# The first stage of a retention and pooling layer: its low-half subtractions on VectorE, GpSimd at rest, context conditioning later

## The chip, the cores and the metric

The kernel runs on one core of a Trainium2 chip. The metric is the device time of one execution in microseconds (us), and a version of the kernel stands for the median of its runs. One execution was also recorded by the hardware profiler. Its engines are named as the profile names them: PE is the matrix engine (PEld its weight loads), DVE is VectorE, ACT is ScalarE, POOL is GpSimd, and SP is the engine that issues the DMAs.

## The reference, cut to what matters

One layer of a diffusion backbone over 512 latent tokens of width 1024, with a context of 256 tokens. The conditioning vectors `c` and `c_ctx` give a shift and a scale for each channel. The normalised tokens and the normalised context are shifted and scaled by them, and multiplied with the input projection:

```python
mod = jax.nn.silu(c) @ w_ada + b_ada
mod_c = jax.nn.silu(c_ctx) @ w_ada + b_ada
...
uc = _modulate(ctx, sh1c, sc1c)
kvc = uc @ w_in[:, :KV_COLS]
s_f, s_b = _context_states(kc, vc, lg)
u = _modulate(x, sh1, sc1)
mix = _token_mixer(u @ w_in, s_f, s_b, lg, pool_w, pool_scale, w_branch_ret, w_branch_pool, w_out)
x = _post_norm(DEEPNORM_ALPHA * x + g1 * mix, ln1_g, ln1_b)
u2 = _modulate(x, sh2, sc2)
x = _post_norm(DEEPNORM_ALPHA * x + g2 * _conv_ffn(...), ln2_g, ln2_b)
```

Of `mod` the first layer norm needs 16 tiles of 128 channels (8 shifts, 8 scales), and the rest of the layer the other 32. Of `mod_c` 16 are needed, from the same 16 tiles of `w_ada`.

## The kernel before

Every product is done with three matmuls. Each operand is held as a high half (the value rounded to the type that TensorE takes, written by ScalarE) and a low half (the value minus its high half, a subtraction on VectorE or GpSimd): high by high, high by low, low by high. All subtractions go through the helper `sub` at line 84. `split` makes both halves of a weight tile: `act.copy` at line 89, then `sub` on the engine that the caller names.

The first stage (lines 257 to 373) has eight steps, one for each block of 128 input channels (kt). A step does the 24 matmuls of line 339 that multiply that block with eight feature tiles: four of q and four of the swish gate. All eight PSUM banks (`g0`) are held until the last step. Before a step, `first_prep` makes its operands for it:

- the weights `w_first[kt]`, loaded into one of three `raw` buffers, are split into `hi` and `lo` (two buffers each);
- `first_mod` computes one shift and one scale tile of `mod`. Each is a `matvec` on VectorE (line 203: a tile of `w_ada`, 128x1024, times silu(c), summed along the row) and a small `finish_mod` (line 206);
- `modulate` (lines 215 to 221) makes the token operand: ScalarE writes the high half `uh` (line 215) and the same in full precision (line 218), and `sub` writes the low half `ul`.

The operands for step kt+1 are made ahead of the matmuls of step kt in the program. In the steps kt=4 to 7, `ctx_mod(0)` to `ctx_mod(3)` follow: each does two such sums (line 226) and two small additions for the context. In this stage all five engines keep the order of the program (`ORDS`).

Then come the steps of `run_steps`: four gate features `g_step` (called g4 to g7 here), the pooling step p0, four steps of k (k0 to k3), p1, four steps of the first half of v, p2, four of the second half, p3, and then the gates and the branches. `run_steps` calls `prep(i + 1)` ahead of the body of step i, so the weights' subtraction for the next step stands before what step i does after its matmuls. From g4 to p0, `ORD0` holds TensorE, SP and VectorE to the order of the program, while ScalarE and GpSimd follow an order chosen by the scheduler when the kernel is built. From k0 on (`ORD1`) only SP keeps the program's order.

The steps g4 to g7 also do, after their matmuls, the last four `ctx_mod`, the swish of the features (`put_g`, lines 378 to 381), the layer norm of the context (bn_stats at line 130, line 417), its transposition (line 137) and `ctx_modulate`, which needs all of them. The steps of k and v need its result. Each of these steps also loads three more tiles of `w_ada` into the `raw` buffers (`ada_tiles`) and multiplies them on VectorE (line 203 again). Their loads share the three `raw` buffers with the weights of the steps.

A pooling step copies its features, and GpSimd adds them up by doubling windows (line 459), multiplies (line 462) and subtracts. Three steps later `middle` makes the halves of the result.

Of the kernel before, what the change touches and what calls it, by code (L numbers as in the profile page):

```python
# [14 lines left out]
P = 128  # L15
# [31 lines left out]
def layer_kernel(ctx: ExitStack, tc: tile.TileContext, a: dict):  # L47
# [38 lines left out]
    def split(raw, shape, eng):  # L86
        hi = sb.tile(list(shape), F32R, tag="hi", bufs=2, name=nm("hi"))
        lo = sb.tile(list(shape), F32R, tag="lo", bufs=2, name=nm("lo"))
        act.copy(hi, raw)  # L89
        sub(eng, lo, raw, hi.bitcast(F32))  # L90
        return hi, lo
# [122 lines left out]
    def modulate(m, sh, sc, src, hi, lo, eng, also=act):  # L214
        act.activation(hi, src, AF.Identity, bias=m[:, sh:sh + 1], scale=m[:, sc:sc + 1])
        u = t2(src.shape)
        if also is act:
            act.activation(u, src, AF.Identity, bias=m[:, sh:sh + 1], scale=m[:, sc:sc + 1])
        else:
            dve.tensor_scalar(u, src, m[:, sc:sc + 1], m[:, sh:sh + 1], ALU.mult, ALU.add)  # L220
        sub(eng, lo, u, hi.bitcast(F32))
# [20 lines left out]
    def first_load(kt):  # L242
        for j in (kt, 8 + kt):
            load(ada_slot(j), a["wada"][j])
        return load(raw4((P, NF0)), a["w_first"][kt])

    def first_mod(kt):
        for j in (kt, 8 + kt):
            matvec(j, ada_slot(j), junk)
            finish_mod(mod, j, j >= 8)  # L250

    def first_prep(kt, raw):
        w = split(raw, (P, NF0), pool)
        first_mod(kt)
        modulate(mod, kt, 8 + kt, xnT[:, kt, :], uh[:, kt, :], ul[:, kt, :], pool)
        return w

    raw0 = first_load(0)
    keep("gap1", [P, 48])
# [82 lines left out]
    for kt in range(NKT):  # L342
        wh, wl = ready
        if kt == 0:
            g0 = [bank() for _ in range(4)]
            g0_mm(kt, range(0, 4), range(2))
            held += [x_trans(2, 1), x_trans(3, 1)]
            g0_mm(kt, range(0, 4), range(2, 3))
            for h in held:
                act.copy(*h)  # L350
            g0 += [bank() for _ in range(N_G0)]
            ready = split(first_load(1), (P, NF0), pool)
            first_mod(1)
            modulate(mod, 1, 9, xnT[:, 1, :], uh[:, 1, :], ul[:, 1, :], pool)
        elif kt + 1 < NKT:
            ready = first_prep(kt + 1, first_load(kt + 1))
        if kt:
            g0_mm(kt, range(0, 4))
        g0_mm(kt, range(4, 4 + N_G0))
        if kt == 1:  # L360
            silu_cc = load(row(), a["c_ctx"].broadcast_to([P, D]))
        elif kt == 2:
            for hf in range(2):
                cs = slice(hf * SEQ, (hf + 1) * SEQ)
                t = t2()
                act.activation(t, silu_cc[:, cs], AF.Sigmoid)
                dve.tensor_tensor(silu_cc[:, cs], silu_cc[:, cs], t, ALU.mult)
        if kt >= 6:
            load(ctx_raw[:, kt - 6, :], a["ctx"][(kt - 6) * P:(kt - 5) * P, :])
        if kt >= 4:  # L370
            ctx_mod(kt - 4)
    ordered(*ORD0)

    qk = slot(0, [P, 2, 4, SEQ])
# [23 lines left out]
    def ctx_trans():  # L398
        for tb in range(2):
            transpose_tb(put_ctxT, ctx_raw[:, tb, :], tb)  # L400

    def ctx_modulate():
        for kt in range(NKT):
            modulate(modc, kt, 8 + kt, ctx_nT[:, kt, :], uch[:, kt, :], ucl[:, kt, :], pool,
                     act if kt % 2 else dve)

    def g_step(h):
        def post(ps):
            if h == N_G0:
                for f in range(4):  # L410
                    act.activation(qT[:, f, :], g0[f], AF.Copy, scale=DK ** -0.5)
                for f in range(2):
                    put_g(f, g0[4 + f])
                ctx_stats = [ln_stats(ctx_raw[:, tb, :]) for tb in range(2)]
                ctx_mod(h)
                for tb, (mu, rs) in enumerate(ctx_stats):
                    dve.tensor_scalar(ctx_raw[:, tb, :], ctx_raw[:, tb, :], mu, rs, ALU.subtract, ALU.mult)
            elif h == N_G0 + 1:
                for f in range(2, N_G0):
                    put_g(f, g0[4 + f])  # L420
                ctx_mod(h)
            elif h == N_G0 + 2:
                ctx_trans()
                ctx_mod(h)
            else:
                ctx_mod(h)
                ctx_modulate()
            put_g(h, ps)

        feature_step(a["w_g"][h - N_G0], NKT, uh, ul, post, pool)  # L430

    rest = list(range(16, 48))

# [10 lines left out]

    def p_step(gi):
        def post(ps):
            invc = load(t2(), a["invc"][gi:gi + 1, :].broadcast_to([P, SEQ]))
            pad = t2((P, PADW))
            pool.memset(pad[:, 0:PADL], 0.0)
            pool.memset(pad[:, PADL + SEQ:PADW], 0.0)  # L450
            act.copy(pad[:, PADL:PADL + SEQ], ps)
            sums = [t2((P, PADW)) for _ in range(2)]
            at, lo, hi, w = pad, 0, PADW, 1
            while w < WINDOWS[gi]:
                nxt = sums[0]
                sums.reverse()
                dl, dr = (1, 0) if w == 1 else (w // 2, w // 2)
                lo, hi = lo + dl, hi - dr
                pool.tensor_tensor(nxt[:, lo:hi], at[:, lo - dl:hi - dl], at[:, lo + dr:hi + dr], ALU.add)
                at, w = nxt, 2 * w  # L460
            d = sums[0][:, 0:SEQ]
            pool.tensor_tensor(d, at[:, PADL:PADL + SEQ], invc, ALU.mult)
            sub(pool, d, d, pad[:, PADL:PADL + SEQ])
            defer(3, middle, d)

        def middle(d):
            dh, dl = t2(dt=F32R), t2(dt=F32R)
            act.copy(dh, d)
            sub(dve, dl, d, dh.bitcast(F32))
            wr = load(small([P, P]), a["pool_w"][gi])  # L470
            pw = t2((P, 2, P), F32R)
            act.copy(pw[:, 0, :], wr)
            sub(dve, pw[:, 1, :], wr, pw[:, 0, :].bitcast(F32))
            defer(1, back, dh, dl, pw)

        def back(dh, dl, pw):
            ps = bank()
            mm3(ps, pw[:, 0, :], pw[:, 1, :], dh, dl, True, True)
            o = t2()
            act.activation(o, ps, AF.Copy, scale=pscale[:, gi:gi + 1])  # L480
            act.copy(poolT[:, 0, gi, :], o)
            sub(dve, poolT[:, 1, gi, :], o, poolT[:, 0, gi, :].bitcast(F32))

        feature_step(a["w_p"][gi], NKT, uh, ul, post, dve)
# [280 lines left out]
    for h in range(N_G0, H):  # L765
        g_step(h)
    p_step(0)
    steps_k = len(steps)
    kv_steps(a["w_k"], True, k_post)
    p_step(1)  # L770
    kv_steps(a["w_v"][0], False, v_post(0))
    p_step(2)
    kv_steps(a["w_v"][1], False, v_post(1))
# [431 lines left out]
```

## Time and profile before

| | us |
|---|---|
| median of three runs | 873.96 |
| the three runs | 1165.45, 870.28, 873.96 |
| the profiled execution | 874.79 |
| its span, from its first instruction to its last | 873.0 |
| busy in the span: PE, DVE, ACT, POOL | 821.6, 624.4, 366.2, 444.2 |

The profiled execution's own time is 1.8 us longer than its span. The granted TensorE clock was 0.981 of full speed over the span. A row of the time line gives start, duration, engine, line, operation, destination and sources, how many instructions were merged, and in square brackets how long the engine had been idle before it and what ended that.

### The profile page before, as it was taken

How to read it: one execution, taken by the hardware profiler on the slowest of the kernel's cores; microseconds unless marked ns; L12 is line 12 of the kernel's file. 1: busy time of each engine (PE TensorE's matmuls, PEld its weight loads, DVE VectorE, ACT ScalarE, POOL GpSimd, SP SyncE). 2: the span in 40 equal slices, each digit the busy share in tenths (PEclk: the TensorE clock that was granted, in tenths of full speed). 3: DMA queues.
4: the chain of work that ended last, by engine and by line, in shares of the span. 5: the costliest groups of instructions: out<-in, count | busy, mean ns of one | idle time of the engine just before them, and what ended most of it. 6: DMA issues, size and time to landing. Idle time of an engine off the chain costs nothing.

```text
span 873.0 us, 10556 instructions
## 1 busy us (share of the span) xinstructions
PE 821.6 (94%) x3865; PEld 678.5 (78%) x3865; DVE 624.4 (72%) x959; ACT 366.2 (42%) x575; POOL 444.2 (51%) x304
## 2 busy tenths in 40 slices
PE   6889989999999999998998899999999998799993
PEld 4667878778888888887787898888888776688883
DVE  7899996676267773346757769999999999612138
ACT  4434544121444343233335476666655565223200
POOL 4877411121543230113456878899888886212245
PEclk9999999999999999999999999999999999999997
DMA  9932466767221104344503312222222252224202
GB/s 352 345 105 94 127 207 218 236 226 216 72 73 49 50 1 145 100 154 163 196 1 121 121 50 84 86 96 99 96 97 95 75 169 83 87 97 144 73 1 96
DMA packets 33780, 106.94 MB, mean 122 GB/s; under 512 B 4528, under 2 KB 5312, under 8 KB 33728
## 3 DMA queue, kind: packets, MB, share of 16 engines
q1 hardware_dynamic: 33728, 106.27, 35.6%
q8 instruction: 30, 0.49, 0.2%
q14 instruction: 22, 0.18, 0.1%
HBM read 104.14 MB, written 2.11 MB: 122 GB/s over the span
## 4 chain that ended last, share of the span: by engine, by line
PE 40%; DVE 39%; POOL 8%; DMA 6%; issue 5%; ACT 2%; SPq 0%; DVEq 0%; POOLq 0%; ACTq 0%
DVE t L938 19%; PE ps L96 11%; PE ps L95 11%; PE ps L94 11%; DVE S L84 4%; DMA raw<-in_wada 4%; DVE t L987 3%; POOL lo L84 3%; DVE raw L203 2%; DVE lo L84 2%; PE ps L339 1%; POOL S L84 1%; POOL sm L123 1%; PE ps L608 1%; DVE sm L130 1%
## 5 line engine op out<-in xcount | busy, mean ns | idle before, releaser
L96 PE MATMUL ps<-S,lo 128*128 128x512 f32 (+1 forms) x544 | 212.2, 392 | 5.1 <-DVE lo L84 4.7
L94 PE MATMUL ps<-S,hi 128*128 128x512 f32 (+1 forms) x544 | 213.6, 393 | 2.7 <-ACT hi L89 2.7
L95 PE MATMUL ps<-S,hi 128*128 128x512 f32 (+1 forms) x544 | 212.5, 391 | 0.2 <-POOL S L84 0.2
L84 POOL TENSOR_TENSOR lo<-raw,hi 128x1024 fp32r<-128x1024 f32 (+1 forms) x53 | 134.0, 2530 | 107.2 <-ACT hi L89 105.3
L938 DVE SCALAR_TENSOR_TENSOR t<-ps,convw,t 128x441 f32<-128x441 f32 (+1 forms) x252 | 167.6, 693 | 15.8 <-POOL t L936 11.5
L89 ACT CAST hi<-raw 128x1024 fp32r<-128x1024 f32 (+1 forms) x98 | 98.9, 1009 | 168.2 <-PE ps L95 61.7
L96 PEld LDWEIGHTS ps<-S,lo 128*128 128x128 f32 x544 | 102.8, 189 | 29.8 <-DVE lo L84 6.8
L94 PEld LDWEIGHTS ps<-S,hi 128*128 128x128 f32 x544 | 103.6, 190 | 23.7 <-ACT hi L89 3.1
L936 POOL TENSOR_TENSOR t<-t,t 128x448 f32<-128x448 f32 x88 | 116.7, 1329 | 10.0 <-ACT t L1013 6.2
L95 PEld LDWEIGHTS ps<-S,hi 128*128 128x128 f32 x544 | 103.7, 191 | 21.3 <-POOL S L84 0.6
L95 PE MATMUL ps<-S,S 128*128 128x512 f32 (+1 forms) x308 | 113.8, 370 | 5.4 <-DVE S L84 5.0
L94 PE MATMUL ps<-S,S 128*128 128x512 f32 (+1 forms) x308 | 113.1, 369 | 3.6 <-DVE t L938 3.6
L96 PE MATMUL ps<-S,S 128*128 128x512 f32 (+1 forms) x308 | 113.8, 370 | 0.2 <-POOL S L84 0.2
L84 DVE TENSOR_TENSOR lo<-raw,hi 128x1024 fp32r<-128x1024 f32 (+1 forms) x47 | 61.4, 1307 | 53.0 <-ACT hi L89 53.0
L84 POOL TENSOR_TENSOR S<-raw,S 128x1024 fp32r<-128x1024 f32 x21 | 50.8, 2423 | 68.7 <-ACT S L735 44.5
L95 PE MATMUL ps<-lo,S 128*128 128x512 f32 x208 | 81.6, 392 | 0.7 <-DVE lo L84 0.6
L96 PE MATMUL ps<-hi,S 128*128 128x512 f32 x208 | 81.3, 391 | 0.0
L94 PE MATMUL ps<-hi,S 128*128 128x512 f32 x208 | 79.2, 392 | 0.0
L95 PEld LDWEIGHTS ps<-S,S 128*128 128x128 f32 x308 | 58.9, 191 | 15.6 <-DVE S L84 5.5
L94 PEld LDWEIGHTS ps<-S,S 128*128 128x128 f32 x308 | 58.6, 191 | 13.6 <-DVE t L938 4.0
L96 PEld LDWEIGHTS ps<-S,S 128*128 128x128 f32 x308 | 58.9, 191 | 10.4 <-POOL S L84 1.1
L84 POOL TENSOR_TENSOR S<-t,S 128x512 fp32r<-128x512 f32 (+1 forms) x29 | 44.8, 1557 | 31.2 <-DVE t L220 11.1
(205 smaller groups left out, 1187.3 us busy)
## 6 DMA issues: line engine op xcount, KB each, us to landing
raw<-in_w_up SPq DMA_DIRECT2D x44, 512.0 KB, 3.3
raw<-in_wada SPq DMA_DIRECT2D x32, 512.0 KB, 4.2
raw<-in_w_down SPq DMA_DIRECT2D x22, 512.0 KB, 3.3
S<-in_wada SPq DMA_DIRECT2D x16, 512.0 KB, 6.8
raw<-in_w_first SPq DMA_DIRECT2D x8, 512.0 KB, 7.4
raw<-in_w_v SPq DMA_DIRECT2D x16, 256.0 KB, 3.3
raw<-in_w_ga SPq DMA_DIRECT2D x8, 512.0 KB, 3.4
raw<-in_w_gb SPq DMA_DIRECT2D x8, 512.0 KB, 3.3
```

The lines of the kernel that those rows point to most:

```text
L84: eng.tensor_tensor(out, x, y, ALU.subtract)
L89: act.copy(hi, raw)
L94: pe.matmul(out, lhsT=sh, rhs=mh, start=first, stop=False)
L95: pe.matmul(out, lhsT=sh, rhs=ml, start=False, stop=False)
L96: pe.matmul(out, lhsT=sl, rhs=mh, start=False, stop=last)
L123: pool.tensor_scalar(rs, mv[:, 1:2], EPS, None, ALU.add)
L130: dve.bn_stats(st[:, hf, :], src[:, hf * SEQ:(hf + 1) * SEQ])
L203: dve.scalar_tensor_tensor(out_junk, raw, 1.0, silu_c, ALU.mult, ALU.mult, accum_out=mod[:, j:j + 1])
L339: pe.matmul(g0[f], lhsT=w[:, f * P:(f + 1) * P], rhs=m[:, kt, :], start=kt == 0 and i == 0, stop=kt == NKT - 1 and i == 2)
L936: pool.tensor_tensor(o, o, i, ALU.add)
L938: dve.scalar_tensor_tensor(o, i, w, o, ALU.mult, ALU.add)
L987: dve.tensor_tensor(accs[2 * f], accs[2 * f], accs[2 * f + 1], ALU.mult)
```

## The change

In the first stage the low half of the weights and the low half of the tokens are both subtracted on VectorE, and the weights' subtraction stands behind `first_mod`. The step kt=0 keeps its own code, with its two half subtractions on GpSimd. The context conditioning `ctx_mod` leaves the first stage and the two gate steps in which it stood alone: two calls each now stand in g4, g6 and g7, and one each in p0 and p1. The context's layer norm moves from g4 to g5, its transposition from g6 to g7. `ctx_modulate` is done in three parts, in g7, p0 and p1. The weights of the gate steps are subtracted on VectorE in place of GpSimd. The pooling step p1 moves ahead of the steps of k, and so into the part where VectorE keeps the order of the program.

```diff
     def first_prep(kt, raw):
-        w = split(raw, (P, NF0), pool)
+        hi = sb.tile([P, NF0], F32R, tag="hi", bufs=2, name=nm("hi"))
+        lo = sb.tile([P, NF0], F32R, tag="lo", bufs=2, name=nm("lo"))
+        act.copy(hi, raw)
         first_mod(kt)
-        modulate(mod, kt, 8 + kt, xnT[:, kt, :], uh[:, kt, :], ul[:, kt, :], pool)
-        return w
+        sub(dve, lo, raw, hi.bitcast(F32))
+        modulate(mod, kt, 8 + kt, xnT[:, kt, :], uh[:, kt, :], ul[:, kt, :], dve)
+        return hi, lo
...
-            ready = split(first_load(1), (P, NF0), pool)
-            first_mod(1)
-            modulate(mod, 1, 9, xnT[:, 1, :], uh[:, 1, :], ul[:, 1, :], pool)
+            ready = first_prep(1, first_load(1))
...
-        if kt >= 4:
-            ctx_mod(kt - 4)
...
-    def ctx_modulate():
-        for kt in range(NKT):
+    def ctx_modulate(kts):
+        for kt in kts:
             modulate(modc, kt, 8 + kt, ctx_nT[:, kt, :], uch[:, kt, :], ucl[:, kt, :], pool,
                      act if kt % 2 else dve)
+
+    def ctx_norm():
+        ctx_stats = [ln_stats(ctx_raw[:, tb, :]) for tb in range(2)]
+        for tb, (mu, rs) in enumerate(ctx_stats):
+            dve.tensor_scalar(ctx_raw[:, tb, :], ctx_raw[:, tb, :], mu, rs, ALU.subtract, ALU.mult)
 
     def g_step(h):
         def post(ps):
             if h == N_G0:
                 for f in range(4):
                     act.activation(qT[:, f, :], g0[f], AF.Copy, scale=DK ** -0.5)
+                ctx_mod(0)
+                ctx_mod(1)
                 for f in range(2):
                     put_g(f, g0[4 + f])
-                ctx_stats = [ln_stats(ctx_raw[:, tb, :]) for tb in range(2)]
-                ctx_mod(h)
-                for tb, (mu, rs) in enumerate(ctx_stats):
-                    dve.tensor_scalar(ctx_raw[:, tb, :], ctx_raw[:, tb, :], mu, rs, ALU.subtract, ALU.mult)
             elif h == N_G0 + 1:
                 for f in range(2, N_G0):
                     put_g(f, g0[4 + f])
-                ctx_mod(h)
+                ctx_norm()
             elif h == N_G0 + 2:
+                ctx_mod(2)
+                ctx_mod(3)
+            else:
                 ctx_trans()
-                ctx_mod(h)
-            else:
-                ctx_mod(h)
-                ctx_modulate()
+                ctx_mod(4)
+                ctx_mod(5)
+                ctx_modulate(range(4))
             put_g(h, ps)
 
-        feature_step(a["w_g"][h - N_G0], NKT, uh, ul, post, pool)
+        feature_step(a["w_g"][h - N_G0], NKT, uh, ul, post, dve)
...
     def p_step(gi):
         def post(ps):
+            if gi < 2:
+                ctx_mod(6 + gi)
+                ctx_modulate((4, 5, 6) if gi == 0 else (7,))
...
     p_step(0)
+    p_step(1)
     steps_k = len(steps)
     kv_steps(a["w_k"], True, k_post)
-    p_step(1)
     kv_steps(a["w_v"][0], False, v_post(0))
```

## Rows read from the trace of the kernel before

**Rows 1.** Busy us of each engine (instructions); last TensorE's clock, DMA share, GB/s.

```profile
24.30:41.96 17.66, 16.78 (x73) 13.04 (x71) 15.37 (x18) 7.24 (x9) 15.67 (x7) 1.00 0.97 357
41.96:73.03 31.07, 24.68 (x96) 18.98 (x97) 30.57 (x43) 12.49 (x17) 21.49 (x8) 0.95 0.28 100
73.03:101.90 28.87, 28.87 (x137) 24.17 (x136) 28.41 (x49) 16.52 (x29) 14.37 (x11) 1.00 0.28 97
```

**Rows 2.** Time line of PE: waits in the first stage, and its end.

```profile
25.06 1.07 PE L339 MATMUL ps<-S,lo 128*128 128x512 f32 x4
44.18 2.01 PE L339 MATMUL ps<-S,hi 128*128 128x512 f32 x4 [2.22 <-ACT S L215]
73.03 0.39 PE L94 MATMUL ps<-S,hi 128*128 128x512 f32 x1
```

**Rows 3.** Groups by line and shape, 19.5 to 73 us: busy, mean ns.

```profile
L203 DVE SCALAR_TENSOR_TENSOR S<-S,row 128x1024 f32<-128x1024 f32 x14 | 30.4, 2173 | 0.0
L84 POOL TENSOR_TENSOR lo<-raw,hi 128x1024 fp32r<-128x1024 f32 x8 | 25.3, 3163 | 3.9 <-ACT hi L89 3.9
```

**Rows 4.** Time line, first stage: sums beside and without GpSimd, ScalarE's modulation.

```profile
26.91 3.38 POOL L84 TENSOR_TENSOR lo<-raw,hi 128x1024 fp32r<-128x1024 f32 x1
28.21 3.17 DVE L203 SCALAR_TENSOR_TENSOR S<-S,row 128x1024 f32<-128x1024 f32 x1
41.80 1.22 DVE L203 SCALAR_TENSOR_TENSOR S<-S,row 128x1024 f32<-128x1024 f32 x1
43.19 1.22 DVE L203 SCALAR_TENSOR_TENSOR S<-S,row 128x1024 f32<-128x1024 f32 x1
43.31 0.81 ACT L215 ACTIVATE S<-S,mod 128x512 fp32r<-128x512 f32 x1 [5.67 <-DVE mod L206]
```

**Rows 5.** Time line: subtractions on VectorE, 1024 wide and 512 wide.

```profile
94.08 1.22 DVE L84 TENSOR_TENSOR lo<-raw,hi 128x1024 fp32r<-128x1024 f32 x1
...
147.38 0.69 DVE L84 TENSOR_TENSOR S<-t,S 128x512 fp32r<-128x512 f32 x1 [1.54 <-ACT S L481]
```

**Rows 6.** Time line: the gate steps' end, first weights, swish, statistics, normalisations.

```profile
89.36 1.91 PE L137 MATMUL ps<-ident,S 128*128 128x128 f32 x16
...
74.66 2.41 POOL L84 TENSOR_TENSOR lo<-raw,hi 128x1024 fp32r<-128x1024 f32 x1 [2.13 <-ACT hi L89]
...
84.08 1.87 DVE L381 TENSOR_TENSOR S<-ps,t 128x512 f32<-128x512 f32 x3
...
74.97 1.28 DVE L130 BATCH_NORM_STATS2 sm<-S 128x6 f32<-128x512 f32 x2
...
8.00 0.76 DVE L277 TENSOR_SCALAR S<-S,sm,sm 128x1024 f32<-128x1024 f32 x1
...
98.00 2.22 DVE L220 TENSOR_SCALAR t<-S,modc 128x256 f32<-128x256 f32 x4
```

**Rows 7.** Time line around k0: a subtraction beside GpSimd, the first wada load.

```profile
102.67 1.62 DVE L84 TENSOR_TENSOR lo<-raw,hi 128x1024 fp32r<-128x1024 f32 x1
...
95.36 0.33 SPq L99 DMA_DIRECT2D raw<-in_wada  x1
```

**Rows 8.** Time line of PE: its two longest waits in k and v.

```profile
129.51 0.72 PE L94 MATMUL ps<-S,hi 128*128 128x512 f32 x1 [2.65 <-ACT hi L89]
...
182.84 0.50 PE L96 MATMUL ps<-S,lo 128*128 128x512 f32 x1 [2.12 <-DVE lo L84]
```

**Rows 9.** The chain that ended last, in order of time, 171 to 177 us.

```profile
171.29 4.45 DMA raw<-in_wada
175.77 1.24 DVE raw L203 x2
```

**Rows 10.** Time line: p1's additions on GpSimd, a sum on VectorE beside them.

```profile
148.92 3.22 POOL L459 TENSOR_TENSOR t<-t 128x527 f32<-128x527 f32 x2 [16.12 <-ACT t L451]
152.22 2.15 POOL L462 TENSOR_TENSOR t<-t,t 128x512 f32<-128x512 f32 x1
...
153.40 2.06 DVE L203 SCALAR_TENSOR_TENSOR raw<-raw,row 128x1024 f32<-128x1024 f32 x1
```

## Prediction

> **What bounds the kernel now.** I read the busy times by stretch first, since the change touches only the first 220 of 873 us. In the first stage TensorE works 16.8 of 17.7 us up to 42 us, then 24.7 of 31.1, and VectorE 30.6 of those 31.1 [rows 1]. Over the gate steps TensorE has no gap, and VectorE is busy 28.4 of 28.9 us [rows 1]. So VectorE is full on both sides, in the second half of the first stage at TensorE's expense.
>
> The time line of PE says what ends TensorE's waits: `uh` from ScalarE, 2.22 us in the worst case [rows 2]. ScalarE had itself idled 5.67 us for VectorE's `finish_mod` [rows 4]. The matmuls behind that wait ran four in 2.01 us, against 1.07 elsewhere [rows 2], and this stretch has the lower mean clock, 0.95 [rows 1]: part of it was at 1.2 GHz and not at 2.4.
>
> Then, why VectorE is slow there. A sum of `first_mod` takes 1.22 us with GpSimd idle, and the next starts 1.39 us after it; beside a weights' subtraction on GpSimd (3.38 us) it takes 3.17 [rows 4]. Over the stage 14 sums average 2.17 us and GpSimd's subtractions 3.16 [rows 3]. The two engines hold each other up.
>
> DMA isn't the bound: its busy share is 0.97 up to 42 us and 0.28 after that [rows 1], so the stage's weights arrive by then, and the last step needs its own at about 50 us.
>
> **First stage.** A matmul comes each 0.227 us where TensorE has no gap: g4 to g6 are 72 of them, from 73.03 to 89.36 [rows 2, 6]. At 25.06 the step kt=1 had four behind it. With its other 20 and six steps of 24 (5.44 us each), TensorE could end at 25.06 + 4.5 + 32.7 = 62.2, against 73.0: 10.8 us to be had.
>
> Does VectorE keep up? Per step it now has two sums (2 x 1.39 = 2.8). Then ScalarE needs 0.1 + 0.8 + 0.8 = 1.7 us for its two passes [rows 4] before VectorE can subtract `ul` (0.69 [rows 5]). The weights' subtraction (1.22 [rows 5]) lies inside that 1.7 and costs nothing. It would cost its 1.2 us if ScalarE's copy to `hi` came late: that copy waits for TensorE to be done with the `hi` of two steps before, and has 2 us to spare by this count. The cycle is 2.8 + 1.7 + 0.7 = 5.2 us against TensorE's 5.44. The swish of c_ctx adds 1.3 us once, which the 0.2 us of slack per step and the lead at kt=1 about cover. So TensorE is the bound by a narrow margin, and the stage's term is **-10.8 us**. The removed context sums (8 at 1.4 us or more) are no gain by themselves: they come back below.
>
> The order of SP's loads in this stage doesn't change; each waits for a `raw` buffer that a VectorE subtraction now frees, earlier than GpSimd did for kt=1 to 3.
>
> **Gate steps and pooling.** Here VectorE, already full, gets 8 more context sums (11.1 us) and four weights' subtractions (4.9 us), in strict order, where a weights' subtraction for the next step stands behind what the step before does after its matmuls. TensorE will wait for it. I follow VectorE's chain. The first weights' subtraction on this path (g5) waits for the `hi` buffer of the stage's last step; in the trace such a one began 1.6 us after the stage's end [rows 2, 6], so 62.2 + 1.6 = 63.8. From there to the end of p1's weights' subtraction stand:
> - the subtractions for g5, g6, g7, p0: 4 x 1.2 = 4.8, and p1's, beside GpSimd's context subtractions, 1.6 [rows 5, 7];
> - 12 context sums, 12 x 1.39 = 16.7 [rows 4];
> - eight products of `put_g`, 8 x 0.62 = 5.0 [rows 6];
> - statistics and normalisation of the context, 2 x 1.28 + 2 x 0.76 = 4.1; two context operations at 0.55, 1.1 [rows 6].
>
> Sum 33.3, so p1's low half is there at 97.1. TensorE does two matmuls of p1 before it needs it and 22 after it (5.0): p1 ends at **102.1**. In the trace of before p0 ends at 89.4 + 1.7 + 10.9 = 102.0 and p1, another 5.4, would end at **107.4**. So 5.3 of the 10.8 us are left; 5.5 go into TensorE's new waits, ahead of g7 and of p1.
>
> The bounds of this term: no cost of GpSimd on p1's subtraction takes 0.4 off; a wait for the two inverse roots on GpSimd ahead of the normalisations, and sums that stretch to 2.06 beside GpSimd [rows 10] in the last two of the twelve, add at most 2.
>
> **Steps of k and v.** What starts here is a ring of three `raw` buffers: load a tile of `w_ada`, sum it on VectorE, load the next. The chain that ended last runs along it, 4.45 us a load and 1.24 a sum [rows 9], and TensorE's wait at 182.84 (2.12 us) is for a subtraction that stands behind such sums [rows 8]. The ring starts when a weights' subtraction frees the first buffer: p0's before, at 95.36 [rows 7]; p1's now, at 97.1, 1.7 us later. It has one load fewer to do ahead of p2, p1's own, worth a third of 4.45 + 1.24, 1.9 us. So by the ring p2 comes when it did before, and nothing is gained; by TensorE all 5.3 us are. p1 was also a step of 5.44 us without sums, in which the loads got ahead, and that is gone from between k and v. On the other hand the wait at 129.51 (2.65 us [rows 8]) is ScalarE's copy of weights late behind the decay tables, no matter of the ring, and while a step's weights wait in a `raw` buffer for TensorE, an earlier TensorE frees it earlier. Neither end is excluded; I take the middle, **+2.7**, as the trace shows one wait of each kind.
>
> **Sum.** -10.8 + 5.5 + 2.7 = -2.6 us. The profiled execution of 874.8 goes to 872.2; the median, 873.96, to **871.4**. Behind 225 us nothing is changed, and TensorE is the bound there, so what is left at that point reaches the end.
>
> **Rivals.**
> - *The gain of the gate steps is carried whole.* TensorE's progress frees the `raw` buffers and the ring follows: 873.96 - 5.3 = 868.7, or 866 if ScalarE's decay tables too stand better. For it: in k, TensorE's wait is not the ring's. Against: at 182.84 it is.
> - *Slower, through the ring.* GpSimd's additions of p1 (3.22 and 2.15 us and more [rows 10]) move from v to k0 and k1, next to p0's. Sums beside them take 2.06 in place of 1.22 [rows 4, 10]: six sums of k0 and k1 cost 5.0 more, two in v get 1.7 back. If the ring also takes the 5.3 us, this is 0 + 3.3: 877.3. It decides where the loads' lead, built up in p1 so far, is used up, in the third or fourth step of v.
> - *VectorE stays as slow as it is.* If the stretched sums are not GpSimd's doing, 14 sums at 2.17 + 0.17, 13.2 us of new subtractions, 2.3 of swish and seven waits of 0.5 from 19.8 end VectorE's part at 71.6, TensorE's at 78.5. That is 16.3 us later than 62.2, and -2.6 becomes about +11 (the ring no more than covers the rest): 885. Against: both sums without GpSimd took 1.22 [rows 4]. The Trainium skill's page "Perfetto Trace Analysis" ("Optimizing Scalar/DVE Operations") speaks for this rival: with VectorE saturated, it has work moved off it, to ScalarE or even GpSimd, and the change does the reverse. The same passage adds that GpSimd and VectorE share a read port, so that an offload between them might not help; "SBUF — State Buffer" ("Who interferes with whom") says it sharper, that a VectorE instruction with two SBUF inputs and a GpSimd instruction that reads SBUF block each other whole. By the first rule it is 885, by the second the sum above; 3.17 beside 1.22 [rows 4] agrees with the second.
> - *Nothing to see*: the terms cancel within half a microsecond, 874.
>
> **How the numbers follow.** Chances: the forecast, 870 to 873, 0.42; carried whole 0.23; the ring slower 0.20; cancelled 0.10; VectorE slow 0.05. From the rivals with their bounds, 865 to 879 leaves out the last and the far ends of two, some 0.15 to 0.2. About 2% (17.5 us) is what a measurement of this kernel tells from no change. To be faster by that it would need more than the whole 10.8 us of the stage; I leave 0.02. Slower by that means over 891, more than the worst case worked out: 0.03.
>
> **What would show it.** In the new profile: no GpSimd subtraction after 20 us in the first stage, sums of `first_mod` near 1.22 us, the first g4 matmul near 62 us. PE waits for VectorE's L84 in g7 and p1, of 2 to 3 us each. p1 done near 102 us. Then waits on L84 or on ScalarE's copies in v, together 2 to 4 us longer than before. Wrong it would be if VectorE's cycle in the first stage exceeds 5.44 us (the margin is 0.2), or if the order that the scheduler builds from k0 on differs, as it may: ScalarE and GpSimd have it from g4 on, VectorE from k0.

## The result and the profile after

| | before | after |
|---|---|---|
| median of 20 runs each, us | 873.93 | 877.80 |
| lowest and highest run, us | 870.28 to 875.50, and one run of 1165.45 | 873.86 to 883.11 |
| the profiled execution, us | 874.79 | 880.45 |
| its span, us | 873.0 | 878.5 |

The ratio is 1.0056, with a 95% interval of 1.0039 to 1.0072. The change makes the kernel about 4 us slower, where 2.6 us faster was predicted. The time lies inside the predicted range, on the side of the rival "slower, through the ring" (877.3). The profiled execution of after is 2.65 us above its median; the places below are those of that execution.

Two places mark the path of TensorE. g4, the first step after the first stage, starts at 73.03 us before [rows 2] and at 62.81 after: 10.2 us earlier. The first matmul of the retention heads, behind everything that the change touches, starts at 229.75 before and at 234.17 after: 4.4 us later. So 14.6 us are lost between the two. Busy time by stretch, with the columns of rows 1:

```profile
24.30:41.96 17.66, 17.66 (x79) 14.62 (x78) 15.62 (x29) 9.82 (x13) 0.00 (x0) 1.00 0.92 351
41.96:62.00 20.04, 20.04 (x90) 16.61 (x89) 14.80 (x25) 10.18 (x14) 0.00 (x0) 1.00 0.48 172
62.00:102.00 40.00, 32.68 (x147) 26.28 (x146) 33.53 (x63) 15.64 (x26) 4.97 (x10) 0.95 0.21 62
102.00:110.00 8.00, 8.00 (x31) 6.41 (x31) 6.52 (x9) 3.07 (x4) 6.38 (x6) 0.83 0.38 146
110.00:225.00 115.00, 104.50 (x444) 83.30 (x443) 82.54 (x171) 33.97 (x69) 16.82 (x17) 0.99 0.64 217
```

The first two lines answer to the first two of rows 1: TensorE has no gap left, GpSimd does nothing, VectorE is no longer full. In the third line TensorE is idle for 7.3 of 40 us, and so is VectorE for 6.5. In the fifth TensorE is idle for 10.5 us.

**First stage.** The groups by line, 19.5 to 63 us, which answer to rows 3, and one turn of VectorE in the time line:

```profile
L203 DVE SCALAR_TENSOR_TENSOR S<-S,row 128x1024 f32<-128x1024 f32 x14 | 17.0, 1217 | 0.0
L84 DVE TENSOR_TENSOR lo<-raw,hi 128x1024 fp32r<-128x1024 f32 x8 | 9.7, 1217 | 1.6 <-ACT hi L89 1.6
```

```profile
46.92 1.22 DVE L203 SCALAR_TENSOR_TENSOR S<-S,row 128x1024 f32<-128x1024 f32 x1
48.31 1.22 DVE L203 SCALAR_TENSOR_TENSOR S<-S,row 128x1024 f32<-128x1024 f32 x1
49.70 1.22 DVE L84 TENSOR_TENSOR lo<-raw,hi 128x1024 fp32r<-128x1024 f32 x1
51.37 0.69 DVE L84 TENSOR_TENSOR S<-t,S 128x512 fp32r<-128x512 f32 x1 [0.46 <-ACT t L218]
51.98 1.22 DVE L203 SCALAR_TENSOR_TENSOR S<-S,row 128x1024 f32<-128x1024 f32 x1
```

All 14 sums take 1.22 us, against a mean of 2.17 before, and the turn is 5.06 us long (46.92 to 51.98), against the 5.44 that TensorE needs for a step.

**Gate steps and p1.** TensorE's waits of over 2 us in this part, and the places where VectorE stands still:

```profile
82.18 0.50 PE L96 MATMUL ps<-S,lo 128*128 128x512 f32 x1 [2.25 <-DVE lo L84]
100.27 0.79 PE L96 MATMUL ps<-S,lo 128*128 128x512 f32 x1 [5.08 <-DVE lo L84]
...
64.39 1.23 DVE L84 TENSOR_TENSOR lo<-raw,hi 128x1024 fp32r<-128x1024 f32 x1 [4.46 <-ACT hi L89]
79.58 0.81 DVE L409 TENSOR_SCALAR S<-S,sm,sm 128x1024 f32<-128x1024 f32 x1 [0.77 <-POOL sm L124]
98.39 0.69 DVE L380 TENSOR_TENSOR S<-ps,t 128x512 f32<-128x512 f32 x1 [2.77 <-ACT t L379]
99.00 1.22 DVE L84 TENSOR_TENSOR lo<-raw,hi 128x1024 fp32r<-128x1024 f32 x1
```

VectorE keeps the program's order. At 98.39 it waits for the swish of g7, and p1's weights (99.00) stand behind that. ScalarE's time line shows why the swish is late: `put_g` of g7 is the last thing in its step, behind the first passes of `ctx_modulate`, which wait for VectorE's context sums.

```profile
94.83 1.09 ACT L215 ACTIVATE S<-S,modc 128x256 fp32r<-128x256 f32 x2 [4.51 <-DVE S L226]
...
96.31 1.08 ACT L215 ACTIVATE S<-S,modc 128x256 fp32r<-128x256 f32 x2
...
97.78 0.57 ACT L379 ACTIVATE t<-ps 128x512 f32<-128x512 f32 x1
```

After its 5.08 us of rest TensorE works at the lower of its two levels, 1.2 GHz, for a while. The stretches of the wait, of the slow matmuls and of the rest of p1:

```profile
97.00:100.27 3.27, 0.00 (x0) 0.00 (x0) 1.88 (x3) 2.83 (x6) 1.70 (x5) 0.62 0.87 152
100.27:104.70 4.43, 4.43 (x11) 3.48 (x12) 3.30 (x8) 1.67 (x3) 1.23 (x2) 0.51 0.77 302
104.70:107.40 2.70, 2.70 (x13) 2.23 (x12) 2.31 (x2) 0.36 (x1) 2.70 (x3) 1.00 0.00 0
```

Of p1's 22 matmuls behind the wait ten start in the first 4.41 us, 0.44 apart, and twelve in the 2.76 us that follow, 0.23 apart (the counts of the windows, 11 and 13, include those that reach over an edge). One row of either kind:

```profile
100.86 0.63 PE L94 MATMUL ps<-S,hi 128*128 128x512 f32 x1
...
104.92 0.40 PE L95 MATMUL ps<-S,hi 128*128 128x512 f32 x1
```

k0 starts at 107.44, where before would stand at 107.4 with p1 in the same place. All of the 10.2 us are gone here.

**k and v.** From k0 to p3 TensorE now has ten waits, together 10.5 us, against three of together 5.4 before (2.65 and 2.12 stand in rows 8, the third is 0.62). The four largest:

```profile
143.89 0.51 PE L94 MATMUL ps<-t,t 128*128 128x512 f32 x1 [0.99 <-ACT t L479]
...
187.46 1.66 PE L94 MATMUL ps<-hi,S 128*128 128x512 f32 x6 [2.55 <-ACT hi L89]
196.91 0.50 PE L95 MATMUL ps<-lo,S 128*128 128x512 f32 x1 [0.77 <-DVE lo L84]
...
217.82 0.80 PE L95 MATMUL ps<-lo,S 128*128 128x512 f32 x1 [3.04 <-DVE lo L84]
```

The chain that ended last shows one turn of the ring here: load the weights, split them, sum two tiles of `w_ada`, and only then is there a buffer for the next weights.

```profile
145.85 4.98 DMA raw<-in_w_v
150.91 1.06 ACT hi L89
151.99 1.23 DVE lo L84
153.21 1.16 DVE raw L203 x2
154.39 0.33 SPq L99
154.77 4.75 DMA raw<-in_w_v
```

From 145.85 to 154.77 that is 8.9 us a turn, while a step of v is 36 matmuls of 0.227, 8.2 us. SP's queue shows how far the loads are; the last row is from the trace of before:

```profile
100.28 11.04 SPq L99 DMA_DIRECT2D raw<-in_wada  x3
...
115.64 11.21 SPq L99 DMA_DIRECT2D raw<-in_wada  x3
...
129.00 6.44 SPq L99 DMA_DIRECT2D raw<-in_wada  x3
136.78 0.80 SPq L99 DMA_DIRECT2D raw<-in_w_v  x2
```

```profile
137.58 0.80 SPq L99 DMA_DIRECT2D raw<-in_w_v  x2
```

Nine tiles of `w_ada` were issued when the first weights of v followed, at 136.78. Before, the first tile goes out at 95.36 [rows 7], and twelve had been issued when the first weights of v followed at 137.58. At nearly the same time the changed kernel is one set of three tiles behind. The program asks for that: SP keeps its order, and with p1 gone from between k3 and v, the first weights of v stand ahead of k3's set.

What the first two sets waited for is in VectorE's time line:

```profile
105.09 1.63 DVE L84 TENSOR_TENSOR lo<-raw,hi 128x1024 fp32r<-128x1024 f32 x1 [1.45 <-ACT hi L89]
106.64 2.08 DVE L226 SCALAR_TENSOR_TENSOR S<-S,row 128x1024 f32<-128x1024 f32 x1
...
108.66 2.31 DVE L84 TENSOR_TENSOR lo<-raw,hi 128x1024 fp32r<-128x1024 f32 x1
...
125.17 0.18 DVE L554 TENSOR_SCALAR t<-t 128x24 f32<-128x24 f32 x1
125.28 1.22 DVE L84 TENSOR_TENSOR lo<-raw,hi 128x1024 fp32r<-128x1024 f32 x1
```

In the first set the second and the third tile are issued at 106.75 and 110.99, each within 0.03 us of the end of a weights' subtraction (105.09 and 108.66), and GpSimd's additions run beside these from 105.59 on. The three operations take 6.0 us; three at 1.22 would be 3.7. In the second set the last tile is issued at 126.53, behind the subtraction at 125.28, which VectorE begins only when most of the decay tables' polynomials are done.

### The profile page after: what moved, and what is told of

It reads as the page before. It is cut to its first block, busy times and chain, and to the rows that moved or that the text cites. A ratio compares the mean times of both kernels' runs of the same rounds, so it can differ in the third digit from the quotient of the medians.

```text
span 878.5 us, 10556 instructions
## 1 busy us (share of the span) xinstructions
PE 821.4 (93%) x3865; PEld 678.2 (77%) x3865; DVE 617.8 (70%) x977; ACT 366.0 (42%) x575; POOL 391.9 (45%) x286
## 4 chain that ended last, share of the span: by engine, by line
DVE 42%; PE 41%; DMA 6%; POOL 4%; issue 4%; ACT 2%; SPq 0%; DVEq 0%; POOLq 0%; ACTq 0%
DVE t L945 19%; PE ps L96 11%; PE ps L95 11%; PE ps L94 10%; PE ps L342 5%; DVE S L84 4%; DVE t L994 3%; DVE lo L84 3%; DMA raw<-in_w_v 3%; DVE raw L203 2%; DVE S L226 2%; DMA raw<-in_wada 2%; DVE sm L130 1%; POOL sm L123 1%; PE ps L615 1%
## 5 line engine op out<-in xcount | busy, mean ns | idle before, releaser
L96 PE MATMUL ps<-S,lo 128*128 128x512 f32 (+1 forms) x544 | 211.9, 392 | 10.5 <-DVE lo L84 10.1
L89 ACT CAST hi<-raw 128x1024 fp32r<-128x1024 f32 (+1 forms) x91 | 91.6, 1007 | 194.9 <-PE ps L95 69.9
L84 POOL TENSOR_TENSOR lo<-raw,hi 128x1024 fp32r<-128x1024 f32 (+1 forms) x42 | 101.2, 2411 | 105.8 <-ACT hi L89 103.9
L84 DVE TENSOR_TENSOR lo<-raw,hi 128x1024 fp32r<-128x1024 f32 (+1 forms) x58 | 74.3, 1283 | 65.5 <-ACT hi L89 65.4
L95 PEld LDWEIGHTS ps<-S,S 128*128 128x128 f32 x308 | 59.7, 194 | 15.8 <-DVE S L84 5.5
L94 PEld LDWEIGHTS ps<-S,S 128*128 128x128 f32 x308 | 59.2, 193 | 13.7 <-DVE t L945 4.0
L96 PEld LDWEIGHTS ps<-S,S 128*128 128x128 f32 x308 | 59.6, 193 | 10.5 <-POOL S L84 1.1
L1020 ACT ACTIVATE t<-ps,convw 128x512 f32<-128x512 f32 x84 | 53.3, 682 | 1.4 <-DVE S L84 1.3
```

The lines of the kernel that those rows point to most:

```text
L84: eng.tensor_tensor(out, x, y, ALU.subtract)
L94: pe.matmul(out, lhsT=sh, rhs=mh, start=first, stop=False)
L95: pe.matmul(out, lhsT=sh, rhs=ml, start=False, stop=False)
L96: pe.matmul(out, lhsT=sl, rhs=mh, start=False, stop=last)
L1020: act.activation(hs, src, AF.Copy, scale=convw[:, i, n:n + 1])
```

## The experiments

Every kernel here computes the whole layer, and each is timed against the kernel before on the same chip. "Heads" is the first matmul of the retention heads.

### The late swish, the place of p1, and two tiles for three

`e1_swish_first` is the changed kernel, with g7's swish ahead of the context's work:

```diff
             else:
+                put_g(h, ps)
                 ctx_trans()
                 ctx_mod(4)
                 ctx_mod(5)
                 ctx_modulate(range(4))
+                return
             put_g(h, ps)
```

> Against the changed kernel (877.8 us): in g7 the swish of that step's own features stands ahead of the context's transposition and sums. Theory ring (the steps of k and v are bound by the three raw buffers): VectorE's wait of 2.77 us ahead of p1's weights goes, PE's wait in p1 falls from 5.1 to about 2.3 us and p1 ends 3 to 5 us earlier, but the waits in v grow by most of that; the end moves by 0 to 1.5 us, to 876.5 to 878. Theory gate (the loss is made in g7 and p1, by ScalarE's order and the slow clock after a 5 us wait): the 3 to 5 us reach the end, 873 to 875.

Measured: ratio 1.0058 [1.0035, 1.0080] (879.85 beside 874.60), the same as the changed kernel's and above both ranges. The wait ahead of p1 fell from 5.08 to 1.85 us, and the matmuls behind it kept the full rate, so k0 started at 103.51 and not at 107.44. The heads started at 233.44, only 0.7 us earlier. What was won was lost again on the way to them, most of it at k2, whose wait is 0.37 us in the changed kernel and 2.48 here:

```profile
98.38 0.50 PE L96 MATMUL ps<-S,lo 128*128 128x512 f32 x1 [1.85 <-DVE lo L84]
...
125.85 1.20 PE L96 MATMUL ps<-S,lo 128*128 128x512 f32 x4 [2.48 <-DVE lo L84]
```

So the late swish explains 3.9 us of p1's lateness, and not the result: 3.2 of the 3.9 are lost again behind it.

`e2_p1_after_k` is the changed kernel with p1 where it was, behind k:

```diff
     p_step(0)
-    p_step(1)
     steps_k = len(steps)
     kv_steps(a["w_k"], True, k_post)
+    p_step(1)
...
-            if gi < 2:
-                ctx_mod(6 + gi)
-                ctx_modulate((4, 5, 6) if gi == 0 else (7,))
+            if gi == 0:
+                ctx_mod(6)
+                ctx_mod(7)
+                ctx_modulate((4, 5, 6, 7))
```

> Against the changed kernel: p1 stands between k and v again, and its context work moves to p0. Theory ring: VectorE has the same to do ahead of k0, so k0 starts near 103 instead of 107 with p1 not yet done, but loads get ahead during p1; the waits in v shrink from 8 to about 4 us, end at 874 to 876. Theory gate: TensorE has nothing to do while VectorE does the context, the wait of p1 becomes one as long or longer in k0, and the end is at 878 to 881.

Measured: 1.0055 [1.0034, 1.0075], 878.83 us, in the range of theory gate; the heads start at 229.98 in the profiled execution, one of the two fastest of a wide set (876.4 to 882.5). At the start of k TensorE waits 1.46 us (97.70) and 4.18 (102.61), together more than p1's 5.08, as theory gate had it, and from there to the heads 5.9 us. The place of p1 alone doesn't decide.

`e3_two_tiles` and `e4_before_two_tiles` let each step of k and v take two tiles of `w_ada`, with one in each step of the gate A (and the scaled q of the heads in another buffer, since its row is still in use there), in the changed kernel and in the one before:

```diff
-            ada_tiles(3)
+            ada_tiles(2)
...
-        if h == 0:
-            qds[0] = row()
-        qd = qds[0][:, (h % 2) * SEQ:(h % 2 + 1) * SEQ].rearrange("p (n c) -> p n c", n=NTB)
+        qd = t2((P, NTB, P))
...
             act.activation(sg[0][:, h, :], ps, AF.Sigmoid)
+            ada_tiles(1)
```

> Against the changed kernel: the steps of k and v load and sum two tiles of w_ada each instead of three, and the eight left over go one to each of the eight gate-A steps; the scaled q of the retention heads is held in tiles of the t2 pool instead of one row tile, since the row is still in use there. Theory ring: PE's waits from k0 to p3 (10.5 us in the changed kernel) fall under 4 us, p3 starts 6 to 8 us earlier than at 227.7, the end is at 869 to 872. Theory gate: p3 starts within 2 us of 227.7, end at 876 to 878.

> The kernel before with the same two edits as e3 (two tiles of w_ada in the steps of k and v, one in each gate-A step, scaled q in t2 tiles). Theory ring: of its 5.9 us of PE waits in k, v and p2 the 3 us that are for VectorE's subtraction go, the 2.65 us behind ScalarE's decay tables stay: end at 870 to 872. Theory gate: no change, 873 to 875.

Measured: e3 1.0078 [1.0052, 1.0104], e4 1.0013 [0.9998, 1.0027]. The heads did start earlier, at 227.17 in e3 and at 221.56 in e4, 8.2 us before those of the kernel before. But the last matmuls of the heads in e4 start only 0.2 us earlier (318.74 against 318.96): the moved tiles made waits among the heads, 3.86 us at 266.99 in e3 and 3.71 at 261.25 in e4. The totals say nothing on the ring, since the edit has a price of its own. The expected times failed.

### Buffers of their own for the tiles of w_ada

The ring is taken away without moving any work: the tiles go into four buffers of their own, and the three `raw` buffers are left to the weights.

```diff
     rest = list(range(16, 48))
+    own = slot(1, [P, 4, D])
...
-                raw = load(raw4(), a["wada"][j])
+                raw = load(own[:, j % 4, :], a["wada"][j])
```

`e5_own_buffers` is that in the changed kernel, `e6_before_own_buffers` in the one before, `e7_own_buffers_swish_first` is e5 with e1's edit.

> Against the changed kernel (877.8 us): the tiles of w_ada in the steps of k and v get four buffers of their own, in a slot that is idle between the first stage and the retention heads, so that the three raw buffers hold weights alone. Nothing else is changed. Theory ring (loads wait for a raw buffer): PE's waits from k0 to p3, 10.5 us in the changed kernel, fall under 4 us, and the end is at 868 to 872, below the kernel before. Theory VectorE (the sums and subtractions themselves, or the order in which VectorE stands for them, bound k and v): the waits stay above 7 us and the end is at 875 to 879.

> The kernel before with the same four own buffers for w_ada. Theory ring: of 5.9 us of PE waits in k, v and p2 only the one behind ScalarE's decay tables (2.65 us) stays, the end is at 870 to 872. Theory VectorE: no change, 873 to 876.

> The changed kernel with the four own buffers and with the swish of g7 ahead of the context's work. Theory ring: now that the ring doesn't take it, the 3 to 5 us by which p1 ends earlier reach the end: 3 to 4 us below e5, 865 to 868. Theory VectorE: within 1 us of e5.

Measured, before at 874.94:

| kernel | median | ratio | k0 starts | heads start |
|---|---|---|---|---|
| e5 | 868.81 | 0.9928 [0.9915, 0.9941] | 107.31 | 222.42 |
| e6 | 869.27 | 0.9937 [0.9923, 0.9950] | 102.50, p1 behind k | 222.85 |
| e7 | 868.72 | 0.9933 [0.9921, 0.9945] | 104.16 | 222.83 |

The four buffers take 1.3% off the changed kernel, some 11 us (1.0056 to 0.9928, each against before on its own chip), and 0.6%, 5.7 us, off the one before. e5 is where theory ring had it, and its waits from k0 on fall to 2.6 us. e6 lies 0.7 us below theory ring's range, and the wait that was to stay, behind the decay tables, isn't there: its one wait in k and v is 2.62 us at 107.55, for a subtraction on VectorE. In e5 p1 still waits 5.08 us and k0 starts within 0.2 us of the changed kernel's place; from there to the heads it takes 115.1 us and not 126.7. So the ring costs 11.6 us between these two places: 7.9 in TensorE's waits, the rest in matmuls that ran slower (496 of them keep TensorE busy for 116.2 us in the ring and for 112.5 out of it, at a granted 0.99 and 1.00). With it gone, the change is worth nothing: e5 and e6 are equal within their intervals. The largest waits for a DMA before and after the edit stand in the list of waits, 110 to 225 us. First the changed kernel:

```profile
ACT hi L89 <- DMA raw<-in_w_v: 33.4, 6, 8.2
...
DVE raw L203 <- DMA raw<-in_wada: 13.5, 12, 2.5
...
ACT hi L89 <- DMA raw<-in_w_k: 10.5, 1, 10.5
```

Then the longest of ScalarE's copies in e5, which wait for TensorE now, as they should:

```profile
ACT hi L89 <- PE ps L96: 29.4, 5, 7.1
```

e7 was expected 3 to 4 us below e5 and is not. Its k0 starts 3.1 us earlier; the lead is gone at k2, whose weights' subtraction stands behind the polynomials of the decay tables in VectorE's order:

```profile
125.69 2.08 PE L96 MATMUL ps<-S,lo 128*128 128x512 f32 x4 [2.78 <-DVE lo L84]
```

So without the ring VectorE's order has the next bound ready.

### The parts one by one

`e8_first_stage_alone` is the kernel before with nothing but the new first stage; the context's work stays where it was. `e9_first_stage_own` is e8 with buffers of their own.

```diff
     def first_prep(kt, raw):
-        w = split(raw, (P, NF0), pool)
+        hi = sb.tile([P, NF0], F32R, tag="hi", bufs=2, name=nm("hi"))
+        lo = sb.tile([P, NF0], F32R, tag="lo", bufs=2, name=nm("lo"))
+        act.copy(hi, raw)
         first_mod(kt)
-        modulate(mod, kt, 8 + kt, xnT[:, kt, :], uh[:, kt, :], ul[:, kt, :], pool)
-        return w
+        sub(dve, lo, raw, hi.bitcast(F32))
+        modulate(mod, kt, 8 + kt, xnT[:, kt, :], uh[:, kt, :], ul[:, kt, :], dve)
+        return hi, lo
...
-            ready = split(first_load(1), (P, NF0), pool)
-            first_mod(1)
-            modulate(mod, 1, 9, xnT[:, 1, :], uh[:, 1, :], ul[:, 1, :], pool)
+            ready = first_prep(1, first_load(1))
```

> The kernel before with one part of the change alone: both low halves of a first-stage step on VectorE, in the new order; the context sums stay in steps kt=4 to 7, the gate weights stay on GpSimd, p1 stays behind k. VectorE's cycle is 5.1 us up to kt=4 and 7.9 after it, so TensorE waits about 2.4 us in each of the steps 5 to 7 and g4 starts near 70 us against 73.0. If VectorE's work up to k0 sets the time, its gate steps begin 3 us earlier and the end is at 870 to 872; if TensorE's progress alone counts, and the rest takes any gain back, 873 to 875.

> The first-stage subtractions alone (as e8, 870.7 us) with the four own buffers for w_ada (as e5 and e6). This is the first of three runs that add the parts of the change one by one, with no ring in the way; e6 (869.3 us) is the step before, e5 (868.8 us) has all parts. e8 starts g4 at 69.8 us against 73.5 in e6. Theory parts (the first-stage subtractions gain, what is put into the gate steps loses it): the 3.7 us reach the end, 865 to 866.5, below every kernel so far. Theory floor (k0 to k2 with their decay tables on VectorE and ScalarE set the time whatever comes before): 868.5 to 869.5.

Both came as the first theory of each had it: 870.70 us with g4 at 69.80, and 864.46, half a microsecond below its range. In e8 the heads start at 223.55. So its lead of 3.2 us at g4 isn't lost in the ring: at the heads it is 6.2 us ahead of before, and its median 4.2.

`e12_plus_context` adds the moved context work to e8. It is e2 with the gate steps' weights on GpSimd again:

```diff
-        feature_step(a["w_g"][h - N_G0], NKT, uh, ul, post, dve)
+        feature_step(a["w_g"][h - N_G0], NKT, uh, ul, post, pool)
```

`e10_plus_context_own` is e12 with buffers of their own, and `e11_plus_gate_weights_own` adds to e10 the gate steps' weights on VectorE (it is e2 with buffers of their own).

> e9 with the context sums, norm and conditioning moved as in the change (all of it done in g4 to g7 and p0); the gate weights stay on GpSimd, p1 stays behind k. g4 starts near 62.5 us. Theory parts: VectorE has the 8 moved sums (11.1 us) ahead of k0 in place of in TensorE's shadow, TensorE waits in p0 or k0, end within 1.5 us of e9 on either side, 864.5 to 867.5. Theory floor: 868.5 to 869.5.

> e10 with the gate weights' subtraction on VectorE, as in the change; p1 alone stays behind k. Theory parts: a wait of 2.3 us in g7 appears and VectorE has 3.4 us more to do ahead of k0, end 1.5 to 3 us above e10; putting p1 ahead of k (e5) then costs the rest up to 868.8. Theory floor: 868.5 to 869.5.

> e10 without the own buffers: the change without its gate weights on VectorE and without p1 ahead of k, with the ring of three raw buffers as it was. Between e8 (870.7 us) and e2 (0.55% above the kernel before). Theory parts: the ring takes most of what TensorE is ahead, end at 872 to 876, so that the context's move alone costs 2 to 5 us where the ring binds and little where it doesn't. Theory floor: within 1 us of e8.

Measured, each as a ratio to the kernel before on the same chip (873.47 for e9 to e12):

| parts | in the ring | with own buffers |
|---|---|---|
| before | 1 | 0.9937 (e6) |
| + first stage on VectorE | 0.9953 [0.9941, 0.9965] (e8) | **0.9886** [0.9865, 0.9908] (e9) |
| + context moved | 1.0048 [1.0031, 1.0065] (e12) | 0.9978 [0.9963, 0.9994] (e10) |
| + gate weights on VectorE | 1.0055 [1.0034, 1.0075] (e2) | 0.9938 [0.9918, 0.9958] (e11) |
| + p1 ahead of k: the whole change | 1.0056 [1.0039, 1.0072] | 0.9928 [0.9915, 0.9941] (e5) |

Read downwards, in both columns: the first stage wins about 0.5%, the moved context loses 0.9%, p1's place is worth nothing that can be told. The gate weights on VectorE give 0.4% back in one column and nothing in the other. e9, 864.5 us, is the fastest kernel of the study, 9 us below before. e11 was expected above e10 and is 3.4 us below it. e12, 878.12 us, is above its range: the moved context costs as much with the ring as without it, while it was expected to cost little without.

The stretch from 62 to 102 us says how the context loses. First e9, then e10, with the columns of rows 1:

```profile
62.00:102.00 40.00, 37.54 (x167) 30.38 (x165) 39.50 (x68) 20.60 (x35) 20.82 (x16) 0.96 0.35 121
```

```profile
62.00:102.00 40.00, 36.35 (x161) 29.48 (x159) 24.95 (x51) 13.68 (x22) 10.95 (x8) 0.96 0.26 93
```

VectorE is full in e9 and idle for 15 of 40 us in e10, and TensorE loses time nonetheless. The time line of e10 has the places:

```profile
65.65 1.29 DVE L380 TENSOR_TENSOR S<-ps,t 128x512 f32<-128x512 f32 x2 [5.11 <-ACT t L379]
72.53 1.89 DVE L380 TENSOR_TENSOR S<-ps,t 128x512 f32<-128x512 f32 x3 [5.59 <-ACT t L379]
81.19 0.81 DVE L409 TENSOR_SCALAR S<-S,sm,sm 128x1024 f32<-128x1024 f32 x1 [3.26 <-POOL sm L124]
105.54 0.69 DVE L380 TENSOR_TENSOR S<-ps,t 128x512 f32<-128x512 f32 x1 [5.12 <-ACT t L379]
```

By these rows it is not the amount of VectorE's work that costs but its order: a short product that must wait for TensorE and ScalarE stands ahead of sums that could have run. That is read off the time line of e10; the test of it, below, is on e5. e10 was expected within 1.5 us of e9 and is 7.6 above it; that theory, that the context's work is harmless once the ring is gone, has fallen. In e10 the first four context sums run inside the first stage, although the program has them behind g4 (TensorE waits 1.51 at 42.09 and 0.85 at 49.02). Even so its g4 starts at 65.50, 2.7 us before that of e9, and its heads at 224.70, 5.6 us behind: 8.2 us are lost between the two.

### Two idle places filled

If idle places are the cause, then filling them gives the loss back. In the changed kernel VectorE rests 4.46 us ahead of 64.39. `e13_fill_own` is e5 with the first two `ctx_mod` moved there; `e14_fill` is the same without the own buffers; `e15_fill_swish_own` adds e1's edit to e13, which fills the place at 98.39.

```diff
+    ctx_mod(0)
+    ctx_mod(1)
     ordered(*ORD0)
...
                     act.activation(qT[:, f, :], g0[f], AF.Copy, scale=DK ** -0.5)
-                ctx_mod(0)
-                ctx_mod(1)
                 for f in range(2):
```

> The changed kernel with the four own buffers (e5, 868.8 us), and the first four context sums taken from behind g4 to the end of the first stage, ahead of the gate weights, where VectorE stood idle for 4.5 us. VectorE does the same work. Theory order (the loss is VectorE's idle time in its fixed order): all that follows on VectorE comes 4 us earlier, PE's wait in p1 falls from 5.1 to about 1 us, end at 864 to 866. Theory amount (the moved sums cost their time wherever they stand): within 1.5 us of e5.

> The changed kernel (877.8 us) with the same four sums at the end of the first stage, with the three raw buffers as they were. Theory order with the ring: p1 ends some 4 us earlier, the ring takes half or more of it, 874 to 877. Theory amount: 877 to 879.

> e13 with the swish of g7 ahead of the context's work as well (as in e7), which fills the second idle place, 2.8 us ahead of p1's weights. Theory order: another 1 to 3 us below e13, 862 to 865. Theory amount: as e5 and e7, 867.5 to 870; e7 showed no gain from this edit alone.

Measured, before at 874.51:

| kernel | median | ratio | k0 starts | heads start |
|---|---|---|---|---|
| e13 | 866.67 | 0.9907 [0.9891, 0.9923] | 104.78 | 219.99 |
| e14 | 878.12 | 1.0040 [1.0026, 1.0055] | 104.10 | 233.37 |
| e15 | 865.47 | 0.9890 [0.9873, 0.9908] | 99.83 | 218.79 |

e13 gained 2.1 of the 4 us expected and misses its range by 0.7: g4 still starts at 62.58, the wait at g7 is gone, the 5.09 us ahead of p1 are still there, and not 1. With the second place filled too, e15 is at e9's ratio, 0.5 us above its range: both halves of the change can be had without loss, if the order is right and the ring is gone. VectorE does the same work in e5 and e15, and the intervals of their ratios lie apart, so the order is worth 0.4%. e14 is the counter-test: k0 0.7 us earlier than in e13, and the heads 13.4 us later; by its time it could be theory amount as well, and the marks decide. In the ring neither edit is worth anything that matters. In e14 the loss is not in longer waits: from k0 to the heads TensorE waits 9.8 us, after 10.5, but its matmuls take 119.4 us where after's take 116.2, at a granted 0.96 and 0.99.

## Why the prediction was wrong

**The first stage** went as predicted. g4 at 62.8 for 62.2, sums at 1.22 us, a turn of 5.06 for 5.2, no GpSimd, no wait of TensorE: 10.2 us for 10.8. The rival "VectorE stays slow" is out: what stretched the sums was GpSimd. The Trainium skill's "SBUF — State Buffer" ("Who interferes with whom") has a VectorE instruction with two SBUF inputs contend with a GpSimd instruction that reads SBUF, and the trace agrees: with GpSimd silent, 1217 ns a sum in place of 2173 [rows 3]. The Trainium skill's "Perfetto Trace Analysis" ("Optimizing Scalar/DVE Operations") says that moving work off a saturated VectorE may make sense, and adds that between VectorE and GpSimd it might not help; e8, 0.47% faster by moving work from GpSimd onto the saturated VectorE, bears out the second half.

**Gate steps and pooling: +5.5 was mis-sized.** p1 was to end at 102.1 and ended at 107.4. The waits stood where they were foretold, at g7 (2.25) and p1, but p1's was 5.08. The chain of 33.3 us added up VectorE's instructions as if it ran without a stop. It had the product of g7's swish but not the wait for it, 2.77 us because of ScalarE's order, and the wait for the root on GpSimd, 0.77, only in the bounds. The chain took 35.8 us, from 64.39 to 100.22, and began 0.6 later than predicted, so p1's low half came 3.1 us after the 97.1 predicted (the waits are longer than the 2.5 us in between: the instructions themselves were priced 1 us too high). And it priced the 22 matmuls behind the wait at 5.0 us, where they took 7.2, ten of them at the lower clock. That is 5.3 us, the whole gain that was to leave this part.

**Steps of k and v: +2.7 was mis-sized too, and its mechanism failed.** It was the middle between "the ring follows TensorE" and "the ring sets the end"; the runs show the second. After has no lead at k0 (107.44, before with p1 taken into account 107.4) and loses 4.4 us from there to the heads, since TensorE's waits grow from 5.4 to 10.5 us. With a lead of 3.9 us (e1) or 3.3 us (e14) at k0 the heads come at 233.44 and 233.37, hardly earlier than 234.17. Out of the ring the same stretch takes 115.1 us and not 126.7 (e5). The first load of a tile came at 100.28, 4.9 us later than before and not 1.7, since it waits for p1's subtraction; the first two sets took 11 us each, and three tiles were missing at the first weights of v. The rival "slower, through the ring" named the mechanism, with 3.3 us, at 877.3; it was given 0.20. Its own price, GpSimd's additions beside k0 and k1, shows in the first set, where an estimate from the rows above is 2.4 us (6.0 less 3.7); in the second set the last load stands behind the decay tables on VectorE. No run takes the additions away by themselves: e2, which moves p1 back, also moves the rest of VectorE's order.

The sum of the measured terms, -10.2 + 10.2 + 4.4, is +4.4 by the marks, and the medians differ by 3.9. The gate steps' term was off by 4.7 and that of k and v by 1.7. In the sum the first error alone turns the sign (-10.8 + 10.2 + 2.7 is +2.1), the second alone doesn't (-10.8 + 5.5 + 4.4 is -0.9). But in e1 the first term is all but put right, with k0 at 103.51 for 102.1, and the time is no better: the ring's term would then have been the larger one.

**What the forecast could not see** is that its two failed terms hide each other. Mending the first alone (e1, e14) does nothing. In e14 the lead is lost to the ring, since e13, the same without the ring, carries its own to the heads; in e1 most of it goes at k2, to VectorE's order, as in e7 without the ring. Mending the second alone (e5) leaves the change equal to before with the same mend (e6). Both mended (e15) are worth 0.5% more than e6, as much as the first stage alone (e9).

## What to carry to other kernels

Work moved to an engine that keeps the program's order can cost more by the idle places that it makes than by its length: look for the instruction that waits on another engine, and see what stands behind it. Where weights and other loads share a few buffers, ask whose work frees a buffer: time won ahead of the ring can be lost in it (e14), though it need not be (e8), and here a few buffers of their own were worth more (0.6 to 1.3%) than the whole rearrangement. When a change has several parts, time the parts alone: here one part won 0.5% and another lost 0.9%.

## What was not expected of the hardware

- After TensorE had rested for 5.08 us, ten matmuls started in 4.41 us at a granted 0.51 of full speed, and the twelve behind them in 2.76 at 1.00. In e1, after a rest of 1.85 us in the same place, the matmuls kept the full rate. So a wait of 5 us cost about 7. The length of the rest alone doesn't tell: in the changed kernel the clock stayed at 1.00 after rests of 2.25 us (82.18) and 2.55 us (187.46), in the kernel before it was 0.52 after 2.22 us (44.18) and after 2.65 us (129.51).
- Some of the kernels differ more from run to run: 873.9 to 883.1 us for the changed kernel in 20 runs, 868.0 to 869.9 for e5 in 5. The ring is not shown to be the reason: e10, without it, ranges from 869.7 to 874.1 in 12 runs, and e12, with it, from 876.7 to 879.5 in 7.
